# Hybrid decoder trunk, first token tiles: norm weight as one row, spread by two products over two PSUM banks

## Chip, cores and metric

One Trainium2 chip, one core. The metric is device time in microseconds of one execution, as the median of three runs. The engines are named as the profile names them: PE is TensorE (PEld its weight loads), DVE is VectorE, ACT is ScalarE, POOL is GpSimd, SP is SyncE. SBUF is the core's working memory, PSUM (eight banks of 128 x 512 float32) takes TensorE's results. Every engine works its own instructions off in order; semaphores make one wait for another.

## The reference, cut

```
for layer in range(2):
    h = rms_norm(x, norm_w[layer])                 # x: 256 tokens x 1024
    proj = einsum('bsd,de->bse', h, w_in[layer])   # 1024 x 12832
    ...
    x = x + einsum('bsd,de->bse', merged, w_out[layer])
return rms_norm(x, final_norm_w)

def rms_norm(x, w):
    return x * rsqrt(mean(x * x, axis=-1) + 1e-6) * w
```

Between the input projection and the output projection stand three mixers (a state-space scan, windowed attention, attention with forget gates). The change touches only the first layer's `rms_norm` and what leads from it to the first products of the projection.

## The kernel before

**Precision.** Dense products run in TensorE's faster float32 form. Each operand is split into a high part (a copy to that form) and a low part (the operand less its high part), and three products replace one: high x high, low x high, high x low. So every weight that is loaded needs one ScalarE copy (high) and one subtraction (low); tokens need the same.

**Tokens.** 256 tokens are two tiles of 128 rows, `x0[:, 0]` and `x0[:, 1]`, 1024 columns each, in two halves of 512. A tile is normalised, turned by TensorE against the identity matrix (four 128 x 128 turns into one PSUM bank for each half, line 278), and split out of that bank: high part by ScalarE (line 268), low part by VectorE (line 269). The results, `hTh` and `hTl`, hold eight k-steps of 128 channels; the first half gives k-steps 0 to 3, the second one 4 to 7.

**Weights.** The weights of a projection come as pieces of 256 or 512 columns. A piece of 256 columns has two parts of four k-steps, each one transfer of 512 KB into a `raw` buffer (line 345, on SyncE's queue; six buffers). The first two pieces belong to the keys and values of the windowed attention. Their four parts are split in pairs of k-steps (128 x 512): both high parts by ScalarE (line 1225), the first pair's low part by VectorE, the second pair's by GpSimd (line 1226, `tt` and `gtt`). Later parts are split whole (128 x 1024, lines 268 and 269, from a call of `split`).

**The start, lines 1211 to 1258.** Under `manual_schedule` the instructions of TensorE, VectorE, ScalarE and GpSimd keep the order in which the program issues them; the trace before shows them in that order. TensorE first does 30 turns of the identity (`WARM`, line 1215). The first tile's squares are summed in two halves, on VectorE (line 1231) and ScalarE (`sum_sq`, line 219). The root is GpSimd's power to -0.5 with one correcting step on VectorE (`rsqrt`, lines 204 to 214). VectorE scales the first tile by root and norm weight (line 1237) and it is turned. The second tile goes another way: ScalarE sums both halves of squares, GpSimd multiplies by the norm weight (lines 1239 and 1245), ScalarE scales by the root (lines 1251 and 1253).

**The first products.** `dense` (line 282) with `after` runs the first tile's 24 products of piece one in two groups of twelve, k-steps 0 to 3 and 4 to 7; in a group first the four high x high, then the four with the tokens' low part, then the four with the weights' low part. After each group of twelve it calls `second_rows(j)` (line 1246), which turns and splits half j of the second tile and then splits one part of piece two (`next(w1)`). The second tile's 24 products follow, k-step by k-step, three products each; then piece two for both tiles. From the third operation on only TensorE's order is by hand.

**Queues.** SyncE issues, in order: first tile (line 162), the norm weight copied to 128 rows (line 163), second tile (line 164), then six weight parts (line 1212, from line 345), and each further part when a raw buffer is free. ScalarE's own queue first has the table load for Exp (line 159).

Of the kernel before, what the change touches and what calls it, by code (L numbers as in the profile page):

```python
# [44 lines left out]
def hybrid_trunk(  # L45
# [17 lines left out]
    def T(tag, shape, dtype=F32, bufs=None):  # L63
        count[0] += 1
        return sb.tile(shape, dtype, tag=tag, name=f"{tag}_{count[0]}",
                       bufs=bufs if bufs is not None else BUFS.get(tag, 1))
# [32 lines left out]
    def transpose(o, a, i):  # L99
        clock["t"] += 0.109  # L100
        nc.tensor.transpose(o, a, i)  # L101
# [52 lines left out]
            print("drained", br, left, "at", round(clock["t"], 1))  # L154


    tab = T("tab", [P, 1])
    nc.vector.memset(tab, 0.0)
    act(tab, tab, AF.Exp)
    x0 = T("L8", [P, 2, D])  # L160
    nwb0 = T("nwb", [P, D])
    nc.sync.dma_start(x0[:, 0, :], x2[0:P, :])
    nc.sync.dma_start(nwb0, norm_w[0:1, :].to_broadcast([P, D]))  # L163
    nc.sync.dma_start(x0[:, 1, :], x2[P:S, :])
    ident = T("ident", [P, P])
    make_identity(nc, ident)
    tri = T("tri", [P, P])
# [36 lines left out]
    def rsqrt(v, n):  # L204

        r0 = T("sm", [P, 8])
        nc.gpsimd.tensor_tensor(r0[:, :n], v[:, :n], mhalf[:, :n], op=ALU.pow)
        a = T("sm", [P, 8])
        tt(a[:, :n], r0[:, :n], r0[:, :n], op=ALU.mult)
        tt(a[:, :n], a[:, :n], v[:, :n], op=ALU.mult)  # L210
        ts(a[:, :n], a[:, :n], -0.5, 1.5, op0=ALU.mult, op1=ALU.add)
        r = T("rs", [P, 8], bufs=4)
        tt(r[:, :n], r0[:, :n], a[:, :n], op=ALU.mult)
        return r
# [19 lines left out]
        stt(r[:, 0:1], a[:, 0:1], -3.0, r0[:, 0:1], op0=ALU.add, op1=ALU.mult)  # L234
        return r

    def row_rstd(ss, n):
        return rsqrt(row_var(ss, n), 1)

# [165 lines left out]
        y.l = l  # L405
        layers.append(y)
    y0 = layers[0]
    y0.nwb = nwb0

    pdma = pin(nc.scalar.dma_start)  # L410

# [682 lines left out]
            pump()  # L1094

    fin = {}

    def hT(y, t):
        if t == 0:
# [16 lines left out]
    def op(i, *fs):  # L1116
        for f in fs:
            ops.append((i, f))

    for y in layers:  # L1120
        l = y.l
        w = w_in[l]
        y.gate, y.qT, y.ckT, y.sz, y.yh, y.yl, y.sq, y.h, y.ss, y.var, y.zdone, y.cqdone = {}, {}, {}, {}, {}, {}, [], {}, {}, {}, set(), {}

        def cols(c0, n=256):
            return sub([(0, w[:, c0:c0 + n])], n)

        def z1(c0, br, b):
            op(cols(c0 + 256 * b), u_z(y, br, 2 * b, 0), u_z(y, br, 2 * b + 1, P))

        def zs(c0, br):
            for b in range(4):
                z1(c0, br, b)

        def gates_proj(br):
            def g(b):
                c = 512 * b
                op(cols(C_G + D * br + c, 512), u_gate(y, br, c, 0), u_gate(y, br, c, 1))

# [12 lines left out]
            return [lambda f=f, b=b: f(b) for f, b in seq]  # L1152

        if l == 0:
            k, v = cols(C_BK), cols(C_BV)
            op(k, u_bkv(y, 0, 0, [lambda j=j: second_rows(j) for j in range(2)]))
            op(k, u_bkv(y, 0, 1))
            op(v, u_bkv(y, 256, 0), u_bkv(y, 256, 1))
            op(None, lambda: layer_consts(y0))
            for c in (0, 2):  # L1160
                op(cols(C_BQ + 256 * c, 512), u_bq(y, c, 0), u_bq(y, c, 1))
        else:
            kv, q0 = cols(C_BK, 512), cols(C_BQ)
# [12 lines left out]
        gp = gates_proj(1)  # L1176
        lights = [lambda: None, lambda: op(cols(C_CV, 512), u_cv(y, 0, 0), u_cv(y, 0, 1))]
        lights += [lambda: None, lambda: op(cols(C_CV + 512, 512), u_cv(y, 512, 0), u_cv(y, 512, 1))]
        lights += [gp.pop(0), lambda: None, gp.pop(0), lambda: None]
        for (c0, u), light in zip(heavy, lights):  # L1180
            op(cols(c0), u_conv(y, u, 0), u_conv(y, u + 1, P))
            light()
        for f in gp:
            f()

        for b, zb in enumerate(((), (0,), (1,), (2, 3))):
            op(cols(C_CK + 256 * b), u_ck(y, 2 * b, 0), u_ck(y, 2 * b + 1, P))
# [23 lines left out]
    with tc.manual_schedule(engines={ENG.PE, ENG.DVE, ENG.Activation, ENG.Pool}):  # L1211
        load_to(N_RAW)
        warm = pmx()
        for i in range(WARM):
            transpose(warm[:, 0:P], ident, ident)
        ss = [T("ss", [P, 4], bufs=4) for _ in range(2)]
        h = [T("L4", [P, D]) for _ in range(2)]
        y0.hTh = T("L8", [P, NK // 2, 2, 2 * P], F32R)
        y0.hTl = T("L8", [P, NK // 2, 2, 2 * P], F32R)
        def shared():  # L1220
            for _ in range(2):
                raw, hi, lo = new_part()
                for k, sub_ in ((0, tt), (2, gtt)):
                    ks = slice(k, k + 2)
                    act(hi[:, ks, :], raw[:, ks, :], AF.Copy)  # L1225
                    sub_(lo[:, ks, :], raw[:, ks, :], hi[:, ks, :].bitcast(F32), op=ALU.subtract)  # L1226
                yield
        w0, w1 = shared(), shared()
        half = (slice(0, 512), slice(512, D))
        junk = T("L2", [P, 512])  # L1230
        nc.vector.tensor_tensor_reduce(out=junk, in0=x0[:, 0, half[1]], in1=x0[:, 0, half[1]], scale=1.0,
                                       scalar=0.0, op0=ALU.mult, op1=ALU.add, accum_out=ss[0][:, 1:2])
        sum_sq(x0, 0, 0, ss[0][:, 0:1], 512)
        r0 = row_rstd(ss[0], 2)
        sum_sq(x0, 1, 0, ss[1][:, 0:1], 512)
        for sl in half:
            stt(h[0][:, sl], x0[:, 0, sl], r0[:, 0:1], y0.nwb[:, sl], op0=ALU.mult, op1=ALU.mult)  # L1237
        sum_sq(x0, 1, 512, ss[1][:, 1:2], 512)
        gtt(h[1][:, half[0]], x0[:, 1, half[0]], y0.nwb[:, half[0]], op=ALU.mult)
        v1 = row_var(ss[1], 2)  # L1240
        to_hT(h[0], 0, y0.hTh, y0.hTl, (0,))
        r1 = rsqrt(v1, 1)
        next(w0)
        to_hT(h[0], 0, y0.hTh, y0.hTl, (1,))
        gtt(h[1][:, half[1]], x0[:, 1, half[1]], y0.nwb[:, half[1]], op=ALU.mult)
        def second_rows(j):
            with tc.high_priority():
                to_hT(h[1], 1, y0.hTh, y0.hTl, (j,))
            next(w1)

        act(h[1][:, half[0]], h[1][:, half[0]], AF.Copy, scale=r1[:, 0:1])
        next(w0)
        act(h[1][:, half[1]], h[1][:, half[1]], AF.Copy, scale=r1[:, 0:1])
        for i, f, _ in ops[:2]:
            f(pieces[i])
        pieces[0].last = True
        release(pieces[0], 2)
        run_op(*ops[2])
# [35 lines left out]
```

## Time and profile before

| | us |
|---|---|
| median of 3 runs (lowest to highest) | 832.72 (832.42 to 832.81) |
| the profiled execution: its time | 832.96 |
| the profiled execution: its span | 831.2 |
| TensorE busy in the span | 819.1 |
| VectorE, ScalarE, GpSimd busy | 654.2, 504.2, 121.1 |

A row of the timeline reads: start, duration from the first start to the last end, engine, line, operation, output <- inputs, shape, count (neighbours of one kind are merged), and in brackets how long the engine was idle before and what released it. A row of windows reads: stretch and its length, then busy time and count for PE, PEld, DVE, ACT and POOL, the granted clock of TensorE, the share of the transfer engines, GB/s. A row of a tile or line reads: line, engine, operation, count, then shortest, median and longest in ns, first and last start, forms. Records of matmuls are pipelined, and their ends are modelled. SPq and ACTq are the queues from which transfers are issued; the last figure of such a row on the page is the time from issue to landing.

### The profile page before, as it was taken

Reading aid. Unit: us, or ns where it says so; the run is one execution under the profiler, and the core shown is the slowest. Engines: PE = TensorE matmul, PEld = TensorE weight load, DVE = VectorE, ACT = ScalarE, POOL = GpSimd, SP = SyncE. Lnnn points to the kernel's source line nnn. Section 1 sums busy time; section 2 is a strip of 40 time slices with the busy share of each in tenths; the row PEclk is TensorE's granted clock in tenths of the full one; section 3 lists DMA queues with packets and bytes.
Section 4 is the critical chain, followed back from the end, with each engine's and each line's share of the span. In section 5 each row is a group of like instructions: output and inputs, shape, how many; then the busy total and the mean of one; then the engine's idle time right before and its main releaser. Section 6 shows DMA issues by size and latency. Waiting matters only on the chain.

```text
span 831.2 us, 15603 instructions
## 1 busy us (share of the span) xinstructions
PE 819.1 (99%) x5788; PEld 745.2 (90%) x5788; DVE 654.2 (79%) x1331; ACT 504.2 (61%) x972; POOL 121.1 (15%) x161
## 2 busy tenths in 40 slices
PE   7999999999999999999999999999999999999996
PEld 7999888989999998888989998898899999888896
DVE  5888987998776678875778889889968667888665
ACT  6566777655666676543555677775557666645442
POOL 7411300000130201100014131000003110021000
PEclk9999999999999999999999999999999999999999
DMA  9945565567474756675687465465756554577632
GB/s 301 275 146 184 179 203 165 171 222 222 134 208 133 247 165 191 215 227 191 210 242 218 148 212 172 144 188 200 239 167 182 173 178 153 167 224 230 215 104 74
DMA packets 123739, 158.39 MB, mean 191 GB/s; under 512 B 12800, under 2 KB 84208, under 8 KB 123664
## 3 DMA queue, kind: packets, MB, share of 16 engines
q1 hardware_dynamic: 109456, 140.79, 53.8%
q10 hardware_dynamic: 14160, 16.49, 6.5%
q8 instruction: 45, 0.74, 0.4%
q14 instruction: 30, 0.25, 0.1%
q0 software_dynamic: 48, 0.13, 0.0%
HBM read 155.22 MB, written 2.16 MB: 189 GB/s over the span
## 4 chain that ended last, share of the span: by engine, by line
PE 96%; DMA 2%; DVE 1%; issue 0%; ACT 0%; POOL 0%; SPq 0%; POOLq 0%; DVEq 0%
PE mm L97 81%; PE mx L97 11%; PE mx L101 4%; DMA raw<-in_w_in_dram 1%; DMA L<-in_x_dram 1%; POOL lo L1226 0%; DVE L L269 0%; DVE lo L269 0%; ACT hi L1225 0%; DVE L L1067 0%; ACT L L219 0%; ACT L L1084 0%; ACT L L268 0%; POOLq L1290 0%; SPq L163 0%
## 5 line engine op out<-in xcount | busy, mean ns | idle before, releaser
L269 DVE TENSOR_TENSOR lo<-raw,hi 128x1024 fp32r<-128x1024 f32 x252 | 309.9, 1244 | 71.8 <-ACT hi L268 69.4
L97 PE MATMUL mm<-hi,L 128*128 128x512 f32 (+1 forms) x1280 | 354.0, 363 | 2.1 <-ACT hi L1225 1.5
L97 PE MATMUL mm<-L,hi 128*128 128x256 f32 x1792 | 316.9, 278 | 0.0
L268 ACT ACTIVATE hi<-raw 128x1024 fp32r<-128x1024 f32 x252 | 263.1, 1055 | 78.2 <-PE mm L97 72.8
L97 PEld LDWEIGHTS mm<-L,hi 128*128 128x128 f32 x1792 | 277.5, 192 | 6.3 <-issue 3.7
L97 PEld LDWEIGHTS mm<-hi,L 128*128 128x128 f32 x1280 | 228.8, 189 | 32.1 <-issue 3.2
L97 PE MATMUL mm<-L,lo 128*128 128x256 f32 x896 | 246.4, 275 | 0.0
L97 PE MATMUL mm<-lo,L 128*128 128x512 f32 (+1 forms) x640 | 229.1, 359 | 1.4 <-POOL lo L1226 1.4
L97 PEld LDWEIGHTS mm<-L,lo 128*128 128x128 f32 x896 | 171.9, 192 | 0.2
L97 PEld LDWEIGHTS mm<-lo,L 128*128 128x128 f32 x640 | 120.9, 189 | 15.5 <-POOL lo L1226 1.8
L925 POOL TENSOR_SCALAR_AFFINE_SELECT bias<-bias 128x128 f32<-128x128 f32 x64 | 39.0, 642 | 268.2 <-DMA bias<-cumd 94.8
L779 DVE SCALAR_TENSOR_TENSOR L<-L,vec,L 128x255 f32<-128x255 f32 (+2 forms) x96 | 46.8, 487 | 6.9 <-ACT L L776 5.5
L949 ACT ACTIVATE L<-L 128x512 f32<-128x512 f32 x24 | 15.1, 630 | 38.9 <-DVE L L948 38.7
L97 PE MATMUL mx<-L,L 128*64 128x128 f32 (+1 forms) x384 | 36.5, 332 | 0.0
L97 PEld LDWEIGHTS mx<-L,L 128*64 128x64 f32 x384 | 23.8, 136 | 11.9 <-issue 2.7
L576 ACT ACTIVATE pp<-pp,nm 128x128 f32<-128x128 f32 x64 | 28.2, 443 | 8.3 <-DVE nm L570 8.3
L651 ACT ACTIVATE pp<-pp,nm 128x128 f32<-128x128 f32 x64 | 25.2, 394 | 12.9 <-DVE nm L644 12.8
L840 ACT ACTIVATE L<-mm 128x256 f32<-128x256 f32 x48 | 18.0, 375 | 20.5 <-PE mm L97 20.3
L782 ACT ACTIVATE L<-L 128x256 f32<-128x256 f32 x32 | 13.3, 416 | 24.4 <-DVE L L779 24.1
L676 POOL TENSOR_SCALAR_AFFINE_SELECT L<-L 128x256 f32<-128x256 f32 x16 | 10.2, 640 | 113.9 <-ACT L L674 113.9
L644 DVE CUSTOM_DVE_ANT_0 pp<-mx,wmask,nsink 128x128 f32<-128x128 f32 x64 | 24.2, 413 | 2.6 <-PE mx L97 2.6
L101 PE MATMUL mx<-ident,L 128*128 128x128 f32 x148 | 22.5, 275 | 0.3 <-DVE L L1237 0.3
(182 smaller groups left out, 795.9 us busy)
## 6 DMA issues: line engine op xcount, KB each, us to landing
raw<-in_w_in_dram SPq DMA_DIRECT2D x200, 512.0 KB, 4.6
raw<-in_w_proj_dram SPq DMA_DIRECT2D x48, 512.0 KB, 5.0
raw<-in_w_out_dram SPq DMA_DIRECT2D x16, 512.0 KB, 4.7
L<-cumd ACTq DMA_DIRECT2D x8, 512.0 KB, 3.7
bias<-cumd ACTq DMA_DIRECT2D x16, 256.0 KB, 3.6
L<-in_gate_bias_dram ACTq DMA_DIRECT2D x12, 256.0 KB, 3.7
L<-in_x_dram SPq DMA_DIRECT2D x2, 512.0 KB, 4.9
nwb<-in_norm_w_dram SPq DMA_DIRECT2D x1, 512.0 KB, 5.4
```

Of the source, the lines that this page charges most:

```text
L97: nc.tensor.matmul(o, a, b, **kw)
L101: nc.tensor.transpose(o, a, i)
L268: keep(act)(hi, src, AF.Copy)
L269: keep(tt)(lo, src, hi.bitcast(F32), op=ALU.subtract)
L576: act(pp[:, i, sl], pp[:, i, sl], AF.Exp, scale=-1.0, bias=nm[:, e:e + 1], accum_out=sums[:, e:e + 1])
L644: nc.vector.tensor_tensor_reduce(out=pp[:, i, sl], in0=score(p, i, b), in1=m, scale=-0.125, scalar=ns[:, i:i + 1], op0=ALU.add, op1=ALU.mi ...
L651: act(pp[:, i, sl], pp[:, i, sl], AF.Exp, scale=-1.0, bias=nm[:, e:e + 1], accum_out=sums[:, e:e + 1])
L779: stt(a[:, s:S], x_[:, 0:S - s], y.vec[:, 16 * j + u:16 * j + u + 1], a[:, s:S], op0=ALU.mult, op1=ALU.add)
L782: act(th, a, AF.Tanh)
L840: act(halves(th), p, AF.Tanh, scale=0.5)
L925: nc.gpsimd.affine_select(out=bias[:, i, dst], in_=bias[:, i, src], compare_op=ALU.is_ge, fill=NEG, base=0, pattern=[[-1, P]], channel_mul ...
L949: act(g, g, AF.Tanh, scale=0.5)
```

## The change

The norm weight of layer 0 arrives as one row of 1024 (4 KB), on ScalarE's queue, ahead of the table load. Behind the 30 turns TensorE multiplies a row of ones (1 x 128) with each half of it (1 x 512), in plain float32, into two PSUM banks `nwp`, so that all 128 rows hold the weight. VectorE reads it there when it scales, in place, and it scales both tiles now (`scaled`). GpSimd's and ScalarE's work on the second tile goes; the second tile's squares are summed by ScalarE and VectorE, as the first's. The epsilon enters with VectorE's sum of squares, and the root has one operation less ahead of the power and one less behind it. The second tile's transfer comes directly behind the first's. The order is written out: both halves of the first tile, its squares and root, then the second tile's squares, parts one and two of piece one, the second root, the second tile's scaling. Nothing happens after the first group of twelve products; after the second group `second_tile` turns both halves, and issues on ScalarE the high part of half one, the four copies of piece two's two parts, and the high part of half two; on VectorE both low parts of the tokens, and then piece two's low parts with GpSimd. `load_to(N_RAW + 2)` issues two more weight transfers ahead of these.

```diff
+    row = T("nwb", [P, D])
+    nc.scalar.dma_start(row[0:1, :], norm_w[0:1, :])
+    x0 = T("L8", [P, 2, D])
+    nc.sync.dma_start(x0[:, 0, :], x2[0:P, :])
+    nc.sync.dma_start(x0[:, 1, :], x2[P:S, :])
     tab = T("tab", [P, 1])
     nc.vector.memset(tab, 0.0)
     act(tab, tab, AF.Exp)
-    x0 = T("L8", [P, 2, D])
-    nwb0 = T("nwb", [P, D])
-    nc.sync.dma_start(x0[:, 0, :], x2[0:P, :])
-    nc.sync.dma_start(nwb0, norm_w[0:1, :].to_broadcast([P, D]))
-    nc.sync.dma_start(x0[:, 1, :], x2[P:S, :])
...
+    def first_root(ss):
+        v = T("sm", [P, 8])
+        ts(v[:, 0:1], ss[:, 0:1], ss[:, 1:2], 1.0 / D, op0=ALU.add, op1=ALU.mult)
+        r0 = T("sm", [P, 8])
+        nc.gpsimd.tensor_tensor(r0[:, 0:1], v[:, 0:1], mhalf[:, 0:1], op=ALU.pow)
+        return v, r0
+    def last_root(v, r0):
+        a = T("sm", [P, 8])
+        stt(a[:, 0:1], r0[:, 0:1], v[:, 0:1], r0[:, 0:1], op0=ALU.mult, op1=ALU.mult)
+        ts(a[:, 0:1], a[:, 0:1], -0.5, 1.5, op0=ALU.mult, op1=ALU.add)
+        r = T("rs", [P, 8], bufs=4)
+        tt(r[:, 0:1], r0[:, 0:1], a[:, 0:1], op=ALU.mult)
+        return r
...
-            op(k, u_bkv(y, 0, 0, [lambda j=j: second_rows(j) for j in range(2)]))
+            op(k, u_bkv(y, 0, 0, [lambda j=j: between[j]() for j in range(2)]))
...
+        nwp = [pmx() for _ in range(2)]
+        for p, sl in zip(nwp, half):
+            mm(p, ones[0:1, :], row[0:1, sl], start=True, stop=True)
...
+        def squares(t):
+            sum_sq(x0, t, 0, ss[t][:, 0:1], 512)
+            nc.vector.tensor_tensor_reduce(out=junk, in0=x0[:, t, half[1]], in1=x0[:, t, half[1]], scale=1.0,
+                                           scalar=D * EPS, op0=ALU.mult, op1=ALU.add,
+                                           accum_out=ss[t][:, 1:2])
+        def part():
+            raw, hi, lo = new_part()
+            def high(k):
+                act(hi[:, k:k + 2, :], raw[:, k:k + 2, :], AF.Copy)
+            def low(k, sub_):
+                sub_(lo[:, k:k + 2, :], raw[:, k:k + 2, :], hi[:, k:k + 2, :].bitcast(F32), op=ALU.subtract)
+            return high, low
+        def turned(t, j):
+            p = pmx()
+            for k in range(4):
+                transpose(p[:, k * P:(k + 1) * P], x0[:, t, j * 512 + k * P:j * 512 + (k + 1) * P], ident)
+            pv = p.rearrange("p (a t) -> p a t", a=2)
+            h, l = y0.hTh[:, 2 * j:2 * j + 2, t, :], y0.hTl[:, 2 * j:2 * j + 2, t, :]
+            return (lambda: act(h, pv, AF.Copy)), (lambda: tt(l, pv, h.bitcast(F32), op=ALU.subtract))
+        def scaled(t, j, r):
+            stt(x0[:, t, half[j]], x0[:, t, half[j]], r[:, 0:1], nwp[j], op0=ALU.mult, op1=ALU.mult)
+
+        squares(0)
+        r0 = last_root(*first_root(ss[0]))
+        scaled(0, 0, r0)
+        th0, tl0 = turned(0, 0)
+        scaled(0, 1, r0)
+        th1, tl1 = turned(0, 1)
+        squares(1)
+        h0, l0 = part()
+        h0(0)
+        th0()
+        h0(2)
+        tl0()
+        root = first_root(ss[1])
+        th1()
+        l0(0, tt)
+        l0(2, gtt)
+        h1, l1 = part()
+        h1(0)
+        h1(2)
+        r1 = last_root(*root)
+        tl1()
+        l1(0, tt)
+        l1(2, gtt)
+        scaled(1, 0, r1)
+        scaled(1, 1, r1)
+        low = []
+        def next_parts():
+            load_to(N_RAW + 2)
             for _ in range(2):
+                h, l = part()
+                h(0)
+                h(2)
+                low.append(l)
+        def second_tile():
+            parts = [turned(1, j) for j in range(2)]
+            parts[0][0]()
+            next_parts()
+            parts[1][0]()
+            for j in range(2):
+                parts[j][1]()
+            for l in low:
+                l(0, tt)
+                l(2, gtt)
+        between.extend([lambda: None, second_tile])
```

More of the change, by code (lines that the diff above doesn't have):

```diff
@@ L235, in row_rsqrt2 @@
         return r
-    def row_rstd(ss, n):
-        return rsqrt(row_var(ss, n), 1)
+    def first_root(ss):
[11 more added lines that the diff above has]
+        return r
     def in_turn(ap):
@@ L407, in hybrid_trunk @@
     y0 = layers[0]
-    y0.nwb = nwb0
     pdma = pin(nc.scalar.dma_start)
@@ L1096, in hybrid_trunk @@
     fin = {}
+    between = []
     def hT(y, t):
@@ L1215, in hybrid_trunk @@
             transpose(warm[:, 0:P], ident, ident)
+        half = (slice(0, 512), slice(512, D))
+        nwp = [pmx() for _ in range(2)]
+        for p, sl in zip(nwp, half):
+            mm(p, ones[0:1, :], row[0:1, sl], start=True, stop=True)
         ss = [T("ss", [P, 4], bufs=4) for _ in range(2)]
-        h = [T("L4", [P, D]) for _ in range(2)]
         y0.hTh = T("L8", [P, NK // 2, 2, 2 * P], F32R)
         y0.hTl = T("L8", [P, NK // 2, 2, 2 * P], F32R)
-        def shared():
-            for _ in range(2):
[L1222 to L1249, printed above, removed]
@@ L1251, in hybrid_trunk @@
-        act(h[1][:, half[0]], h[1][:, half[0]], AF.Copy, scale=r1[:, 0:1])
-        next(w0)
-        act(h[1][:, half[1]], h[1][:, half[1]], AF.Copy, scale=r1[:, 0:1])
+        junk = T("L2", [P, 512])
+        def squares(t):
[3 more added lines that the diff above has]
+                                           accum_out=ss[t][:, 1:2])
```

## The prediction

> **What bounds the kernel now.** I read the page's busy shares first, then the chain of waits, then the windows of the span, and last the timeline of the first 20 us, engine by engine.
>
> ```profile
> span 831.2 us, 15603 instructions
> PE 819.1 (99%) x5788; PEld 745.2 (90%) x5788; DVE 654.2 (79%) x1331; ACT 504.2 (61%) x972; POOL 121.1 (15%) x161
> ...
> 10.00:20.00 10.00, 7.85 (x59) 7.18 (x60) 6.54 (x16) 8.54 (x15) 7.80 (x6) 1.00 1.00 337
> 20.00:30.00 10.00, 10.00 (x75) 9.47 (x74) 9.60 (x10) 6.46 (x10) 5.92 (x5) 1.00 0.94 267
> 30.00:60.00 30.00, 30.00 (x198) 27.11 (x197) 22.50 (x65) 17.26 (x44) 7.59 (x8) 1.00 0.60 187
> 60.00:400.00 340.00, 340.00 (x2439) 309.12 (x2438) 272.35 (x545) 210.33 (x400) 40.77 (x54) 1.00 0.60 189
> 400.00:800.00 400.00, 399.45 (x2829) 363.17 (x2828) 322.10 (x651) 246.92 (x476) 51.63 (x67) 1.00 0.63 196
> ```
>
> TensorE is the bound. From 20 to 800 us it is idle for 0.55 us. So whatever the start gains or loses reaches the end one to one, as long as the start only shifts TensorE's queue. The question is when that queue begins to run without a hole. In the chain of waits this is near 17 us:
>
> ```profile
> 2.18 7.81 DMA raw<-in_w_in_dram
> ...
> 10.01 1.16 ACT hi L1225 x2
> ...
> 14.67 1.29 POOL lo L1226
> 15.96 0.04 issue
> 16.00 0.51 PE mm L97 x2
> 16.51 0.43 PE mx L101 x4
> 16.94 8.35 PE mm L97 x72
> ```
>
> The first weights land at 9.99; then ScalarE's high parts and GpSimd's low parts hold TensorE, until the second tile's last turn at 16.35. The last hole of the start is in the second tile's 24 products:
>
> ```profile
> 16.35 0.60 PE L101 MATMUL mx<-ident,L 128*128 128x128 f32 x4
> 16.98 0.60 ACT L268 ACTIVATE L<-mx 128x512 fp32r<-128x512 f32 x1
> 17.48 1.14 ACT L1225 ACTIVATE hi<-raw 128x512 fp32r<-128x512 f32 x2
> 17.61 0.69 DVE L269 TENSOR_TENSOR L<-mx,L 128x512 fp32r<-128x512 f32 x1 [0.34 <-ACT L L268]
> ...
> 18.11 0.28 PE L97 MATMUL mm<-lo,L 128*128 128x256 f32 x1
> 18.23 0.52 PE L97 MATMUL mm<-hi,L 128*128 128x256 f32 x2
> ```
>
> The second half of that tile is turned (16.35), its high part copied (16.98 to 17.58) and its low part formed (to 18.30). The second of the two products at 18.23, the first one that reads that low part, starts 0.28 us (one product's time, the row above it) before the pair's end: 18.23 + 0.52 - 0.28 = 18.47. **My sum is the shift of this instruction**, the product of the second tile's fifth k-step with the tokens' low part; behind it TensorE has all it needs.
>
> **What is removed.** The broadcast norm weight (512 KB, second in SyncE's queue) goes, and 4 KB come on ScalarE's queue.
>
> ```profile
> nwb<-in_norm_w_dram SPq DMA_DIRECT2D x1, 512.0 KB, 5.4
> ...
> 1.24 0.43 SPq L163 DMA_DIRECT2D nwb<-in_norm_w_dram  x1
> ...
> 8.07 0.63 ACT L219 ACTIVATE L<-L 128x512 f32<-128x512 f32 x1 [2.98 <-DMA L<-in_x_dram]
> ```
>
> It landed at 1.24 + 5.4 = 6.64, the second tile at about 8.0. So second tile and weights come some 1.4 us earlier: about 6.6, and 8.6 for the first weights. If that wait stayed the bound, this would be the gain. The issue of the 4 KB stands ahead of ScalarE's table load, whose result is wanted at 4.37 only; cover more than 1.5 us. Even if it took as long as the second tile does now (8.0 - 1.7 = 6.3), it is there at 7.1, before TensorE asks. The two 512 KB issues that are added wait, as the later ones do now, for a raw buffer: nothing. GpSimd's two weight products, one square and two scalings on ScalarE go; none of them is in my chain except through what replaces them.
>
> **The two row products.** They stand behind the 30 warming turns in TensorE's queue.
>
> ```profile
> L101 PE MATMUL mx<-ident x30: 273/417/473, 1.5 to 7.3; 128*128 128x128 f32 x30
> L97 PE MATMUL mx<-L,qt x128: 269/374/378, 52.6 to 527.0; 64*128 64x128 f32 x64, 64*128 64x256 f32 x64
> L97 PE MATMUL mx<-L x32: 272/327/382, 156.6 to 637.8; 128*128 128x256 f32 x16, 128*128 128x128 f32 x16
> 156.48 0.73 PEld L97 LDWEIGHTS mx<-L 128*128 128x128 f32 x4
> 157.14 0.19 PEld L97 LDWEIGHTS mm<-L,hi 128*128 128x128 f32 x1
> ```
>
> The last turn starts at 7.31, so TensorE is free at about 7.42. A full float32 product is two records (line 813 issues 8 products of 256 columns, the group counts 16). Here 256 + 128 columns took 157.14 - 156.48 = 0.66 us, so 512 take 0.88; by the starts of the products instead it is 0.77. Fewer rows do not help as far as the rows show: 64 rows have 378 ns where 128 have 382. A one-row product is in no row; its bounds are 0.2 (as if the rows counted) and 0.88; I take 0.88, the row nearest to it, since half the rows saved nothing. Bank one is done at 8.30. From a product's passage to its reader's start go 0.2: four turns take 0.60 and one at least 0.273, so they start 0.11 apart, the last one at 16.68, passes in 0.11 and is read at 16.98. So **bank one is read at 8.50, bank two at 9.38**.
>
> The first root is ready long before: one small operation of 0.2 less ahead of GpSimd's power and one less behind it, so at 6.6 instead of 7.02 (6.86 + 0.16 below). The banks decide.
>
> ```profile
> 4.37 0.69 DVE L1231 CUSTOM_DVE_ANT_0 L<-L 128x512 f32<-128x512 f32 x1 [3.44 <-DMA L<-in_x_dram]
> 6.86 0.16 DVE L213 TENSOR_TENSOR rs<-sm,sm 128x1 f32<-128x1 f32 x1
> 7.06 1.41 DVE L1237 SCALAR_TENSOR_TENSOR L<-L,rs,nwb 128x512 f32<-128x512 f32 x2
> 9.86 0.55 POOL L207 TENSOR_TENSOR sm<-sm,mhalf 128x1 f32<-128x1 f32 x1 [0.27 <-DVE sm L224]
> ```
>
> **VectorE's line behind the banks**, in program order: scaling (two at 1.41, so 0.66 from start to start and 0.75 each): 8.50 to 9.25 and, with bank two, 9.38 to 10.13. Then the second tile's square, 10.04 to 10.73 (0.69, the first row), which waited behind the scalings though its tokens are there since 6.6. The first low part of the tokens 10.75 to 11.44 (0.69; its high part ends at 10.5: turned 9.31, read 9.94). The variance, 11.36 to 11.51. The weights' low part, first pair, 11.44 to 12.13. Power on GpSimd, asked for at 11.6.
>
> **Where VectorE and GpSimd meet.** These rows price GpSimd's pairs of 512:
>
> ```profile
> 11.18 0.69 DVE L1226 TENSOR_TENSOR lo<-raw,hi 128x512 fp32r<-128x512 f32 x1
> 11.24 1.78 POOL L1226 TENSOR_TENSOR lo<-raw,hi 128x512 fp32r<-128x512 f32 x1 [0.82 <-ACT hi L1225]
> ...
> 12.81 0.76 DVE L1226 TENSOR_TENSOR lo<-raw,hi 128x512 fp32r<-128x512 f32 x1 [0.34 <-ACT hi L1225]
> 12.98 1.73 POOL L1245 TENSOR_TENSOR L<-L,nwb 128x512 f32<-128x512 f32 x1
> 14.67 1.28 POOL L1226 TENSOR_TENSOR lo<-raw,hi 128x512 fp32r<-128x512 f32 x1
> ```
>
> Alone it takes 1.28. With a VectorE operation of two SBUF inputs under way it ends 1.15 after that one (11.87 to 13.02, 13.57 to 14.71). VectorE in its turn started at 12.81, met GpSimd's end at 13.02 and ended 0.55 behind it. They take turns and wait each other out.
>
> Applied here: the power (0.55, of which 1.28 - 1.15 = 0.13 runs before the turn) is asked for during the weights' low part and ends at 12.13 + 0.42 = 12.55. GpSimd goes straight on to the first pair's low part, 12.53 to 13.81, while VectorE has the second root's three small operations next, two of them with two SBUF inputs. The first gets its turn at 13.81, the third waits for GpSimd's next pair, 13.95 to 15.10. Root at 15.2. No row shows so small an operation waiting; the bounds are no wait at all (root at 13.1, three starts of 0.19 behind 12.55) and the whole of both pairs. I take the whole, since the operations of 512 waited whole. Then in VectorE's queue: token low part 15.20 to 15.89, weights' low part to 16.51, scalings of the second tile to 17.18 and 17.84. [...]
>
> **The order behind it.** TensorE's 24 products of the first tile end with the part from 16.51, at 17.0. Then both halves of the second tile are turned, one behind the other, where one was turned in the middle before: first one 17.23, read at 17.86. Now ScalarE: high part, then **four** copies of the next two weight parts, then the other half's high part.
>
> ```profile
> 15.37 0.58 ACT L268 ACTIVATE L<-mx 128x512 fp32r<-128x512 f32 x1
> 15.85 1.14 ACT L1225 ACTIVATE hi<-raw 128x512 fp32r<-128x512 f32 x2
> ```
>
> Starts are 0.48 apart behind a turn's copy, 0.52 within the pair (1.14 - 0.62). So 17.86 + 0.49 + 4 x 0.52 = 20.43; before, two copies lay between. Copied at 21.03, low part 21.06 to 21.75, product 0.17 later: 21.92, against 18.47. **The shift is 3.45 us: 832.96 + 3.45 = 836.4 for a profiled execution**, which stood 0.24 above the median of the runs; so **836.2** as a median. Later demands stay covered: the second piece's low parts are ready at 22.4 and 23.1, TensorE takes them from 23.2; VectorE's three rope operations and GpSimd's two sums move by as much as TensorE does.
>
> **Rivals.**
> *The small operations don't wait.* The root is there at 13.1, the tokens' low part at 13.8, and only the weights' low part and GpSimd's last pair take turns, in one order or the other: the last parts are ready at 15.7 to 16.0, the second tile's first turn starts at 15.9 to 16.4 instead of 17.23, and the shift is 2.1 to 2.6; at 2.4 the time is 835.1. For: no row shows a small one waiting. Against: the operation at 12.81 did.
> *No turns at all in this place.* The power ends at 12.2, GpSimd's pairs take 1.5 each (between 1.28 and 1.78) and end at 15.2, and by the path above the product comes 5.0 later, at 20.2: shift 1.7, 834.4. Against: both orders of waiting stand in the rows.
> *A cheap row product.* At 0.2 each the banks are read at 7.8 and 8.1; the second scaling starts 0.66 behind the first, at 8.5 instead of 9.38. With whole waits the shift is 2.6, 835.3; with no turns 0.8, 833.5. Against it speaks the 64-row row.
> *The earlier weights decide (not slower).* The place is the landing of the first weights, 9.99 now and 8.6 then. It decides if the banks are read before 7.06, where scaling starts today, so that all the work behind them meets its weights 1.4 us earlier: 831.3. For: the chain starts with that DMA. Against: the banks come behind 30 turns that end past 7.3, and ScalarE's queue has the copies ahead of the last high part.
> *More holes.* If TensorE's waits (12.4 to 13.9, 14.7 to 15.9) leave half a microsecond that I don't see, 836.7.
> That the change does nothing can't be: ScalarE's order alone is two copies (1.04 us) longer ahead of the last high part.
>
> **How the numbers follow.** Whole waits 0.43 (836.2), small ones don't wait 0.20 (835.1), no turns 0.13 (834.4), cheap product 0.12 (0.07 of it 835.3, 0.05 of it 833.5), more holes 0.04, earlier weights 0.08 (831.3). A measurement of this kernel tells 0.2% from no change, 1.7 us: 831.1 to 834.4. "No turns" lies on that edge and is halved; "earlier weights" lies 0.2 inside the other and goes 0.05 out, 0.03 in. So slower 0.43 + 0.20 + 0.06 + 0.07 + 0.04 = 0.80, within 0.15, faster 0.05. The range runs from "no turns" with products at 0.77 (834.2, and some of the cheap ones) to more holes with their few tenths: 833.9 to 836.9; outside are the earlier weights and the cheapest case, 0.13, and what lies above.
>
> **What would show it.** Scaling starts at about 8.5, on TensorE, and not at 6.7; the second root's small operations held up until about 15.2, some 2.6 us behind GpSimd's power; GpSimd's two pairs back to back from 12.5; the second tile's second high part at 20.4 on ScalarE behind four copies; TensorE's unbroken run from about 21.9. I am wrong if scaling starts at 7, if the second root takes under 0.7 us behind the power, or if a wait on TensorE beyond 25 us appears.

## The result and the profile after

| | before | after |
|---|---|---|
| median of 6 runs each (lowest to highest), us | 832.78 (832.42 to 833.05) | 836.15 (835.90 to 836.42) |
| the profiled execution: time, span, us | 832.96, 831.2 | 836.0, 834.2 |

The changed kernel takes 1.0041 of the time before, with an interval of 1.0031 to 1.005; the medians differ by 3.4 us, the two spans by 3.0. Of all runs below one is set apart, a run of experiment 3 that took 1423.32 us at a mean granted clock of 0.557; that row's highest time and ratio leave it out. The head of the page and the windows of the changed kernel (stretch, length, busy time and count of PE, PEld, DVE, ACT, POOL, granted clock, share of the transfer engines, GB/s):

```profile
span 834.2 us, 15604 instructions
...
10.00:20.00 10.00, 7.58 (x41) 6.39 (x40) 6.71 (x11) 4.06 (x9) 4.12 (x4) 0.83 0.76 257
...
60.00:400.00 340.00, 340.00 (x2436) 308.95 (x2435) 272.91 (x552) 212.41 (x411) 39.66 (x54) 1.00 0.62 191
400.00:800.00 400.00, 399.51 (x2843) 363.61 (x2843) 323.09 (x652) 246.82 (x476) 51.71 (x67) 1.00 0.63 194
```

From 60 to 800 us TensorE is idle for 0.49 us, where it was 0.55 before. So nothing was lost late, and the whole difference lies in the start. One number was not there before: a mean granted clock of 0.83 between 10 and 20 us, where the kernel before had 1.00 in its profiled execution. The timeline of the start, all engines, with the rows that answer to the prediction's steps (start, duration, engine, line, operation, output <- inputs, shape, count, idle time before and its releaser):

```profile
1.51 4.93 PE L101 MATMUL mx<-ident 128*128 128x128 f32 x30 [1.51 <-POOL ident masks.py:199]
6.37 1.98 PE L97 MATMUL mx<-nwb,ones 1*128 1x512 f32 x4
7.40 0.63 ACT L1249 ACTIVATE hi<-raw 128x512 fp32r<-128x512 f32 x1 [0.78 <-DMA raw<-in_w_in_dram]
7.53 1.61 DVE L1264 SCALAR_TENSOR_TENSOR L<-L,rs,mx 128x512 f32<-128x512 f32 x2 [0.51 <-PE mx L97]
9.68 1.49 PE L97 MATMUL mm<-hi,L 128*128 128x256 f32 x8
10.55 0.93 POOL L242 TENSOR_TENSOR sm<-sm,mhalf 128x1 f32<-128x1 f32 x1 [4.17 <-DVE sm L240]
11.45 2.54 POOL L1252 TENSOR_TENSOR lo<-raw,hi 128x512 fp32r<-128x512 f32 x2
11.52 1.24 DVE L248 SCALAR_TENSOR_TENSOR sm<-sm,sm 128x1 f32<-128x1 f32 x1 [0.45 <-POOL sm L242]
12.98 1.03 DVE L251 TENSOR_TENSOR rs<-sm,sm 128x1 f32<-128x1 f32 x1
14.67 1.20 PE L97 MATMUL mm<-hi,L 128*128 128x256 f32 x4 [0.89 <-DVE L L1261]
15.14 1.40 DVE L1264 SCALAR_TENSOR_TENSOR L<-L,rs,mx 128x512 f32<-128x512 f32 x2
15.67 1.05 PE L97 MATMUL mm<-lo,L 128*128 128x256 f32 x4
16.52 1.83 PE L101 MATMUL mx<-ident,L 128*128 128x128 f32 x8
17.61 0.60 ACT L1261 ACTIVATE L<-mx 128x512 fp32r<-128x512 f32 x1 [5.94 <-PE mx L101]
18.11 2.18 ACT L1249 ACTIVATE hi<-raw 128x512 fp32r<-128x512 f32 x4
20.18 0.58 ACT L1261 ACTIVATE L<-mx 128x512 fp32r<-128x512 f32 x1
21.55 0.39 PE L97 MATMUL mm<-hi,L 128*128 128x256 f32 x1 [0.34 <-DVE L L1261]
```

Read it from the bottom. The product that the prediction followed starts at 21.55, against 18.47 before: a shift of 3.08 for a span that grew by 3.0. It waits for the second low part of the second tile on VectorE, and that for the high part (20.18), which stands behind four copies (18.11). These stand behind the first high part (17.61) and the turns (16.52). The turns follow the first tile's last eight products in TensorE's queue (14.67, 15.67); the scaling (15.14) is done with its first half at about 15.9 and doesn't hold them. The eight products wait 0.89 us for a low part of the tokens, which stands on VectorE behind the second root, and two of that root's three small operations last 1.24 and 1.03 us while GpSimd works on its two pairs (11.45 to 13.99). The first weights (7.40) are there well before TensorE can use them.

The clock has its own rows, in windows of half a microsecond (length, PE busy and count of records, granted clock, share of the transfer engines, GB/s):

```profile
4.00:4.50 0.50, 0.50 (x4) 1.00 0.99 401
4.50:5.00 0.50, 0.50 (x7) 1.00 0.96 383
...
14.50:15.00 0.50, 0.33 (x1) 0.73 0.99 344
...
18.00:18.50 0.50, 0.50 (x4) 0.85 0.26 94
```

A window whose clock is 0.73, between 1.00 and 0.50, was at half pace for 54% of its length. The windows left out have 1.00 up to 14.5 and 0.50 from 15.0 to 18.0. So the fall is at 14.73, and by the same reckoning the rise is at 18.15: 3.42 us at half pace, right where the second tile is turned.

### The profile page after: what moved, and what is told of

Same layout as the page of the kernel before. It is cut to its first block, busy times and chain, and to the rows that moved or that the text cites. A ratio compares the mean times of both kernels' runs of the same rounds, so it can differ in the third digit from the quotient of the medians.

```text
span 834.2 us, 15604 instructions
## 1 busy us (share of the span) xinstructions
PE 822.2 (99%) x5792; PEld 746.3 (89%) x5792; DVE 657.6 (79%) x1331; ACT 502.3 (60%) x968; POOL 116.6 (14%) x159
## 3 DMA queue, kind: packets, MB, share of 16 engines
HBM read 154.70 MB, written 2.16 MB: 188 GB/s over the span
## 4 chain that ended last, share of the span: by engine, by line
PE 97%; DVE 1%; issue 1%; ACT 0%; DMA 0%; POOL 0%; POOLq 0%; DVEq 0%
PE mm L97 82%; PE mx L97 11%; PE mx L101 4%; DMA L<-in_x_dram 0%; DVE L L1261 0%; POOL sm L242 0%; DVE sm L248 0%; ACT L L1261 0%; ACT hi L1249 0%; ACT L L1097 0%; DVE L L283 0%; DVE L L1241 0%; ACT L L282 0%; POOLq L1349 0%; ACT L L219 0%
## 5 line engine op out<-in xcount | busy, mean ns | idle before, releaser
L97 PEld LDWEIGHTS mm<-lo,L 128*128 128x128 f32 x640 | 121.2, 190 | 15.2 <-POOL lo L1252 1.4
```

Source lines behind the costliest of these rows:

```text
L97: nc.tensor.matmul(o, a, b, **kw)
```

## The experiments

Edits 1 to 8 are made to the changed kernel, 9 and 10 to the kernel of 8; each has 4 to 11 runs. Three groups of them (1 to 4, 5 to 8, 9 to 11) each stood beside the kernel before on their own chip; its median there was 832.65, 832.79 and 832.64 us, so the groups can be laid side by side. The profiles below are of one execution each, and the place of the half clock and the time at which the banks are read differ from one to the next: what an edit gains is read from the medians, and the profile shows which wait is gone.

| | median, us (lowest to highest) | ratio to before | interval |
|---|---|---|---|
| the change | 836.15 (835.90 to 836.42) | 1.0041 | 1.0031 to 1.0050 |
| 1 first small operation | 835.09 (834.10 to 835.47) | 1.0026 | 1.0016 to 1.0037 |
| 2 both small operations | 834.98 (834.30 to 835.61) | 1.0027 | 1.0017 to 1.0037 |
| 3 copies last | 834.91 (834.57 to 835.38) | 1.0026 | 1.0016 to 1.0037 |
| 4 filling turns | 835.81 (835.22 to 837.05) | 1.0038 | 1.0023 to 1.0053 |
| 5 earlier root | 834.32 (833.25 to 834.96) | 1.0016 | 1.0007 to 1.0026 |
| 6 = 2 and 3 | 833.85 (833.21 to 834.45) | 1.0012 | 1.0002 to 1.0021 |
| 7 twenty turns | 835.40 (834.82 to 835.74) | 1.0031 | 1.0019 to 1.0042 |
| 8 all in order | 831.53 (830.84 to 832.69) | 0.9985 | 0.9976 to 0.9994 |
| 9 = 8, 128 rows | 831.18 (830.44 to 832.32) | 0.9982 | 0.9973 to 0.9991 |
| 10 = 8, twenty turns | 832.17 (830.25 to 832.39) | 0.9984 | 0.9975 to 0.9993 |
| 11 = 8 again | 831.07 (830.54 to 832.40) | 0.9983 | 0.9974 to 0.9992 |

The ratio is not the quotient of the two medians; in 10, whose runs fall into two groups, that quotient is 0.9994. The intervals of 1, 2, 3 and 7 overlap that of the change, but none of the runs that they rest on reaches its lowest one, 835.90.

**1. The first small operation without a second tensor.** It multiplies r0 by v and by r0; here both factors come in as one scalar for each row, and only one operand is read as a tensor.

```diff
-        stt(a[:, 0:1], r0[:, 0:1], v[:, 0:1], r0[:, 0:1], op0=ALU.mult, op1=ALU.mult)
+        ts(a[:, 0:1], r0[:, 0:1], v[:, 0:1], r0[:, 0:1], op0=ALU.mult, op1=ALU.mult)
```

> Changed kernel, but the first of the second root's three small VectorE operations has one tensor input and two per-row scalars instead of two tensor inputs. Theory (two SBUF tensor inputs make a VectorE operation wait out GpSimd's pair, however small it is): the first no longer waits (1.24 us now), the third waits for the end of the first pair only, the root is ready at about 12.8 instead of 14.0, the second tile is turned at about 15.2 instead of 16.5: 1.2 to 1.7 us faster than the changed kernel, 834.5 to 834.9. Rival (the operations are late for another reason, the power's result or the pointers): 836.1, the first one still takes 1.2 us.

The timeline of the second root in experiment 1:

```profile
11.93 0.93 POOL L242 TENSOR_TENSOR sm<-sm,mhalf 128x1 f32<-128x1 f32 x1 [5.72 <-DVE sm L240]
12.83 2.55 POOL L1252 TENSOR_TENSOR lo<-raw,hi 128x512 fp32r<-128x512 f32 x2
12.89 0.27 DVE L248 TENSOR_SCALAR sm<-sm,sm 128x1 f32<-128x1 f32 x1 [0.45 <-POOL sm L242]
...
13.38 0.75 DVE L251 TENSOR_TENSOR rs<-sm,sm 128x1 f32<-128x1 f32 x1
```

The same value at the same place, while GpSimd works on its pair: 0.27 where the other form took 1.24. The third operation, left as it was, waits out the first pair only (to 14.13). The root is there 1.27 behind the power's end at 12.86, and not 2.53 as in the change (11.48 to 14.01). In this execution the banks came late (scaling from 8.90), so the times of day are not those of the change. The median fell by about 1 us, a little less than expected. So the waits are real and are paid on the path.

**2. Neither small operation with a second tensor.**

```diff
-        stt(a[:, 0:1], r0[:, 0:1], v[:, 0:1], r0[:, 0:1], op0=ALU.mult, op1=ALU.mult)
+        ts(a[:, 0:1], r0[:, 0:1], v[:, 0:1], r0[:, 0:1], op0=ALU.mult, op1=ALU.mult)
...
-        tt(r[:, 0:1], r0[:, 0:1], a[:, 0:1], op=ALU.mult)
+        ts(r[:, 0:1], r0[:, 0:1], a[:, 0:1], None, op0=ALU.mult)
```

> Changed kernel, with the first and the third of the root's small operations in the form with one tensor input. Theory: none of them waits, root at about 12.0, GpSimd's second pair ends at 14.4, the second tile is turned at 14.9: 2.1 us faster than the changed kernel, 834.0, and TensorE's granted clock may then stay at full. Rival: 836.1.

This was missed by half. The timeline of experiment 2, the power and then VectorE from the third small operation on:

```profile
11.86 0.93 POOL L242 TENSOR_TENSOR sm<-sm,mhalf 128x1 f32<-128x1 f32 x1 [5.54 <-DVE sm L240]
...
13.32 0.21 DVE L251 TENSOR_SCALAR rs<-sm,sm 128x1 f32<-128x1 f32 x1
...
14.05 1.81 DVE L1252 TENSOR_TENSOR lo<-raw,hi 128x512 fp32r<-128x512 f32 x1
15.78 1.39 DVE L1264 SCALAR_TENSOR_TENSOR L<-L,rs,mx 128x512 f32<-128x512 f32 x2
```

The root now takes 0.74 behind the power (12.79 to 13.53). But the weights' low part behind it, 0.68 alone, lasts 1.81: VectorE meets GpSimd's second pair there instead. The scaling starts at 15.78, in experiment 1 at 15.86. The wait had moved by one instruction, so that the second repair brought nothing (834.98 against 835.09). Nor did the clock stay at full: in this execution it is at half from 10.57 to 13.98.

**3. The copies of the next weights behind the second high part.**

```diff
             parts[0][0]()
-            next_parts()
             parts[1][0]()
+            next_parts()
```

> Changed kernel, with the high part of the second tile's second half ahead of the four copies on ScalarE. Theory (the four copies delay the last low part): the high part starts at 18.1 instead of 20.2, the product that needs the last low part at 20.5 instead of 21.55, bounded by TensorE's own pace then: 1.05 us faster, 835.1. Rival (the four copies are needed as early, the later piece is the bound): the wait moves to the second piece's products, 836.1.

ScalarE and TensorE in experiment 3:

```profile
18.43 0.60 ACT L1261 ACTIVATE L<-mx 128x512 fp32r<-128x512 f32 x1 [0.26 <-PE mx L101]
...
18.95 0.39 PE L97 MATMUL mm<-hi,L 128*128 128x256 f32 x1 [0.22 <-DVE L L1261]
...
20.36 0.40 PE L97 MATMUL mm<-hi,L 128*128 128x256 f32 x2
```

The high part that began at 20.18 begins at 18.43, and TensorE has no hole behind 18.95. The time fell by 1.1 to 1.2 us: the order on ScalarE is a cause of its own. It isn't the full 1.75, because TensorE now has the products of four k-steps to do first, from 18.95 on, about as late as in the change. The product that was followed, the second of the two at 20.36, starts at 20.48 (20.36 + 0.40 - 0.28), 1.07 before 21.55, as expected.

**4. Ten turns of the identity in the empty place between the groups of twelve.** They are to keep the clock up.

```diff
-        between.extend([lambda: None, second_tile])
+        def filler():
+            for i in range(10):
+                transpose(warm[:, 0:P], ident, ident)
+
+        between.extend([filler, second_tile])
```

> Changed kernel, with ten more turns of the identity into the spare bank behind the first twelve products, in a hole of TensorE (13.1 to 14.7). Theory (the half clock from 14.8 to 18.2 comes from the hole ahead of it, and costs 1.0 us on the path, as much as the row products came earlier than I put them): the granted clock stays at 1.0, the second tile's turns take 1.0 us instead of 1.8, 835.1. Rival (the half clock comes from something else, or is off the path): 836.1.

The first tile's last four products, the second tile's turns and the product that ends the start, in experiment 4:

```profile
15.60 0.74 PE L97 MATMUL mm<-lo,L 128*128 128x256 f32 x4
16.31 1.33 PE L101 MATMUL mx<-ident,L 128*128 128x128 f32 x8
...
20.91 0.39 PE L97 MATMUL mm<-hi,L 128*128 128x256 f32 x1 [0.34 <-DVE L L1261]
```

In this execution the granted clock was 1.00 in every window of the start; the turns take 1.33 and not 1.83, and the product starts 0.64 earlier than in the change, though the row products start 0.37 later (6.74). The median of four runs is only 0.3 lower, and the interval covers that of the change. So in these two executions the half clock costs time on the path, where it falls on the turns; that filling turns mend it over many executions isn't shown.

**5. The second root ahead of the pairs.**

```diff
-        r0 = last_root(*first_root(ss[0]))
+        root = first_root(ss[0])
+        squares(1)
+        r0 = last_root(*root)
+        root = first_root(ss[1])
         scaled(0, 0, r0)
         th0, tl0 = turned(0, 0)
         scaled(0, 1, r0)
         th1, tl1 = turned(0, 1)
-        squares(1)
+        r1 = last_root(*root)
...
-        root = first_root(ss[1])
...
-        r1 = last_root(*root)
```

> Changed kernel, with the second tile's squares, variance and power ahead of the first tile's scaling, in the hole in which VectorE waits for the row products, and its root's small operations directly behind the scalings. Theory (the wait for the row products costs because the second root stands behind it, and the small operations then meet GpSimd's pairs): no small operation waits, the power is off the path, the second tile is turned at about 14.4 instead of 16.5, 1.8 to 2.4 us faster than the changed kernel: 833.7 to 834.3. Rival (the pairs of 512 alone hold the line): the gain stays at that of the earlier runs, about 1.0, 835.1.

Experiment 5, the operations with unchanged form but another place:

```profile
8.61 1.60 DVE L1264 SCALAR_TENSOR_TENSOR L<-L,rs,mx 128x512 f32<-128x512 f32 x2 [1.43 <-PE mx L97]
10.13 0.21 DVE L248 SCALAR_TENSOR_TENSOR sm<-sm,sm 128x1 f32<-128x1 f32 x1
...
10.56 0.16 DVE L251 TENSOR_TENSOR rs<-sm,sm 128x1 f32<-128x1 f32 x1
...
11.34 1.79 DVE L1252 TENSOR_TENSOR lo<-raw,hi 128x512 fp32r<-128x512 f32 x1
...
15.74 1.33 PE L101 MATMUL mx<-ident,L 128*128 128x128 f32 x8
```

0.21 and 0.16 for the very instructions that took 1.24 and 1.03: it was the meeting that was dear. GpSimd is met again by the weights' low part (1.79), but the turns start at 15.74 and not at 16.52, though the banks came 1.1 later in this execution (scaling from 8.61). Part of that is the clock, which is at full here by then: the turns take 1.33 and not 1.83. The time fell by 1.8 us, in relation to before from 1.0041 to 1.0016.

**6. Experiments 2 and 3 together.**

> Changed kernel with both edits: the root's small operations with one tensor input, and the copies behind the last high part. Theory (two terms, one behind the other on one path): the gains add, 1.2 + 1.2, 833.8. Rival (each uncovers the same other wait): 834.9.

833.85, 2.3 us below the change, where 2 and 3 alone brought some 1.1 each. The causes add up. What is left to before is 1.1 us; no run takes that apart.

**7. Twenty warming turns for thirty.**

```diff
-WARM = 30
+WARM = 20
```

> Changed kernel with 20 warming turns instead of 30, so that the row products stand 10 turns earlier in TensorE's queue. Theory (VectorE's scaling waits for the products alone): scaling starts at the root, 7.05, and bank two is there: 0.6 us faster, 835.5, more where the clock rises late. Rival (with fewer turns the clock rises later and the products run at half speed): scaling starts at 8 to 9, 836.1 or more.

First the scaling, then two windows of TensorE in experiment 7:

```profile
7.28 1.61 DVE L1264 SCALAR_TENSOR_TENSOR L<-L,rs,mx 128x512 f32<-128x512 f32 x2 [0.28 <-PE mx L97]
```

```profile
9.50:10.00 0.50, 0.50 (x4) 0.72 1.09 344
...
16.50:17.00 0.50, 0.50 (x6) 0.95 0.61 164
```

Scaling starts at 7.28, near the theory's 7.05, and the time, 0.8 below that of the change, is near its 835.5. The banks are read 0.25 earlier than in the profile of the change, whose turns sped up early (at some 4.5 us), and 1.62 earlier than in that of experiment 1. Against this the clock is at half from 9.72 to 16.55, which is 6.83 us, twice 3.42, as the rival had it in kind. What each of the two is worth can't be told from this run.

**8. Everything at once.** The small operations as in experiment 2, the second root early, the weights' first low part ahead of it on VectorE, each half of the second tile scaled early and turned behind one of the two groups of twelve as the kernel before did, and the copies of piece two last.

```diff
         h0(0)
+        l0(0, tt)
         th0()
         h0(2)
+        l0(2, gtt)
+        r1 = last_root(*root)
         tl0()
-        root = first_root(ss[1])
+        scaled(1, 0, r1)
         th1()
-        l0(0, tt)
-        l0(2, gtt)
...
+        def first_half():
+            th, tl = turned(1, 0)
+            th()
+            tl()
+
+        def second_half():
+            th, tl = turned(1, 1)
+            th()
+            tl()
             load_to(N_RAW + 2)
...
-        between.extend([lambda: None, second_tile])
+        between.extend([first_half, second_half])
```

> Changed kernel in another order: second root early, small operations with one tensor input, the weights' first low part on VectorE ahead of the root and asked for before GpSimd's, the second tile's first half scaled and turned between the two groups of twelve products, the copies of the second piece last. Theory (every term of the sum is an order, and the row products themselves are cheap): TensorE runs without a hole from about 14.2, the product that stood at 18.47 before the change comes at 15.8: 2.7 us faster than before, 830.0. Rival (the row products' place and the pairs of 512 keep the start as late as before): 832.5.

The windows and TensorE's timeline in experiment 8:

```profile
9.00:9.50 0.50, 0.50 (x4) 0.63 1.09 346
...
12.50:13.00 0.50, 0.50 (x6) 0.95 1.05 385
```

```profile
6.97 1.98 PE L97 MATMUL mx<-nwb,ones 1*128 1x512 f32 x4
...
10.60 2.16 PE L97 MATMUL mm<-hi,L 128*128 128x256 f32 x8
...
13.07 0.60 PE L101 MATMUL mx<-ident,L 128*128 128x128 f32 x4
...
15.32 0.63 PE L101 MATMUL mx<-ident,L 128*128 128x128 f32 x4
```

This kernel beats both: 831.53, and 831.07 when it was run again (11), 1.3 to 1.6 us below before. TensorE is busy all but without a hole from the first products on, and each half is turned behind one group of twelve (13.07, 15.32). The expected time was 1.5 lower. In this execution the clock is at half from 9.13 to 12.55, and the first eight products take 2.16 where eight took 1.49 in the change. That isn't all of it: the runs of 8 and 11 whose clock stood highest still have a median of 830.84, against the 830.0 expected.

**9 to 11. The row products in 128 rows, twenty turns, and the same once more.** In 9 the row stands in a zeroed tile and is multiplied in all 128 rows by ones; 10 has 20 turns, by the edit of 7; 11 is experiment 8 unchanged.

```diff
+    nc.vector.memset(row, 0.0)
...
-            mm(p, ones[0:1, :], row[0:1, sl], start=True, stop=True)
+            mm(p, ones, row[:, sl], start=True, stop=True)
```

> The reordered kernel, with the two row products as products of 128 rows: all rows of the norm weight's tile are zeroed first (VectorE), row 0 is loaded, and the ones have 128 rows. Same two products of 512 columns, same result. Theory (a product of one row keeps TensorE busy in the records, but does not count as work for its clock: in every run with the late rise the half clock follows the row products by one or two us): the granted clock no longer falls to 0.5 between 9 and 13 us, and the first 24 products of the tokens run at full pace: 0.5 to 1.0 faster than the reordered kernel, 830.6 to 831.0. Rival (the fall comes from the hole behind, or zeros count no more than missing rows): the fall stays, 831.5.

> The reordered kernel with 20 warming turns. Theory (VectorE's scaling waits for the products, also in this order): scaling starts at about 7.2 instead of 8.1, 0.4 to 0.9 faster than the reordered kernel, 830.6 to 831.1. Rival (fewer turns leave the clock at half for longer and take it back): 831.5 or more, with granted clock at 0.5 through two windows, as in the run with ten turns less.

> The reordered kernel once more, as the mark for the other two on one chip: 831.5, ratio to the kernel before 0.9985.

The row products in experiment 9, then in experiment 10:

```profile
7.64 1.88 PE L97 MATMUL mx<-nwb,ones 128*128 128x512 f32 x4
```

```profile
5.98 3.77 PE L97 MATMUL mx<-nwb,ones 1*128 1x512 f32 x4
```

128 rows cost 1.88, one row costs 1.98: rows make no difference to the price. To the clock they seem to: each run also gives its mean granted clock over the span (a block of 3.42 us at half lowers it by 0.002, and one can fall into the idle end too, as in the profile of before, which is at 0.50 from 830.0 on). In 8 and 11 together, 8 of 21 runs have 0.995, with a median of 831.77, and 5 have 0.999, with one of 830.84; in 9 all eleven lie between 0.997 and 0.999. This isn't proof: the kernel before, which has no row products, shows 0.995 or 0.996 in 8 of its 27 runs beside them. And the median of 9 is no better, 831.18 against 831.07; why is open. Experiment 10 misses: its runs fall into two groups, five from 830.25 to 831.26 and six from 832.17 to 832.39, and the profiled one, 832.21, has its row products at half pace (3.77, against 1.98 in 8), and the turns ahead of them keep to 4 or 5 records in each half microsecond from 4.0 to their end at about 6.0. That the fewer turns are the cause is the author's estimate: experiment 7, also with twenty, has row products of 2.12.

## Why the prediction was right

| step | predicted | measured |
|---|---|---|
| row products start | 7.42 | 6.37 |
| bank two is read after bank one | 0.88 | 0.86 (7.53 + 1.61 - 0.75 = 8.39) |
| scaling of the first tile | 8.50 | 7.53 |
| root behind the power's end | 2.65 (12.55 to 15.2) | 2.53 (11.48 to 14.01) |
| scaling of the second tile | 16.51 | 15.14 |
| its first turn, first copy | 17.23, 17.86 | 16.52, 17.61 |
| second high part behind the first | 2.57 | 2.57 (17.61 to 20.18) |
| the product that ends the start | 21.92 | 21.55 |
| shift of it | 3.45 | 3.08 |

**The small operations.** They wait, and for the whole pair each (1.24 and 1.03 us, against 0.21 and 0.16 in experiment 5): the choice that the prediction made between bounds of nothing and both pairs. Experiment 1 takes one of the waits away by its form, experiment 5 both by their place, and the time falls with them. With two tensors the first operation of 128 x 1 took 1.24 while GpSimd worked on its pair; with one tensor and two scalars it took 0.27 at the same place. But what the waits cost is not their sum. Experiment 2 shows that the next operation with two SBUF inputs waits in their place (1.81, against 0.68 alone), and 1.2 us are gained (836.15 to 834.98). The prediction's rival of small ones that don't wait had this price, 1.1 (836.2 to 835.1), since it let the low part take turns with GpSimd; the expectation for experiment 2 did not.

**The copies on ScalarE.** Step and size were right, 0.49 + 4 x 0.52; experiment 3 shows that they are on the path.

**The row products.** One row costs as much as 128 (1.98 and 1.88 for the two products), as taken, so the rival of a cheap one falls. Their start was off for this execution: "TensorE is free at about 7.42" was read from one execution, and in the profile of the change the turns sped up at some 4.5 us, in that of before at some 7.0. So the banks, and all that follows on VectorE down to the root, came about 1 us earlier than put, and scaling at 7.53 is nearer to the prediction's own sign of being wrong (7) than to its 8.5. In experiments 1, 2 and 5, which leave the turns and the row products as they were, it begins at 8.90, 8.84 and 8.61. So this start moves from execution to execution, and one trace can't give it.

**The clock.** It isn't in the sum; the rival of more holes put half a microsecond for something unseen. The half clock from 14.73 to 18.15 holds up the first tile's last products and the second tile's turns. Four products with the weights' low part take 1.05 (0.74 at full pace in experiment 4), and from the second tile's first turn to its copy go 1.09, where the prediction took 0.63. The path differs there too: in the prediction the first turn waits for the scaling (16.51 to 17.23), in the profile for these products. Against the prediction the second tile's scaling comes 1.37 early, the copy behind its turns only 0.25: some 1.1 us of the lead are gone in between, most of it by the clock. So in this execution two errors of about 1 us each nearly cancelled, and 836.2 was as close to 836.15 as it was partly by luck. The two big terms, waits and copies, were not luck: experiment 6 takes off what these two edits can reach of both, and 2.3 of the 3.4 us go with them.

**The earlier weights.** They came at 7.40 (at 8.48 in experiment 2), earlier than the 8.6 put, and TensorE's first products stood behind other work, so the side on which the change could have been faster never came into reach. Experiment 8, without the waits, the copies and the late turns in the second tile's path, is 1.3 to 1.6 us faster than before, about as much as the weights were put earlier (1.4). That this is their saving isn't shown: no run gives the kernel before the new order and leaves its weights where they were.

## What to carry to other kernels

A transfer that comes earlier is worth what the queue behind it can use (here the copy of the first weights started at 7.40 instead of 10.01, and the kernel took 3.4 us longer): list the instructions that stand between it and the bound engine, in program order, and price each at the place where it now falls. Look for VectorE's operations with two SBUF tensors in the time in which GpSimd works, the small ones too: here one of 128 x 1 took 1.24 us there and 0.21 elsewhere, and 0.27 there with its other operands as scalars for each row; then look which instruction meets GpSimd next. Copies for the next piece belong behind the last piece of work that the bound engine is waiting for (experiment 3: 836.15 to 834.91).

## What was not expected of the hardware

In these traces the granted clock goes in blocks of 3.42 us. In the profile of the change it falls at 14.73 and rises at 18.15; counted back by 3.42 this gives 11.31, 7.89 and 4.47, and at about 4.5 the warming turns double their pace (4 records in the window from 4.0, 7 in that from 4.5), though the recorded clock says 1.00 on both sides. In experiment 7 it is at half for two blocks (9.72 to 16.55), in 8 for one (9.13 to 12.55). In the block ahead of the fall in the change, 11.31 to 14.73, TensorE worked for 1.36 of 3.42 us (to 11.62, 12.79 to 13.78, and 0.06 at the end, behind a wait of 0.89). TensorE's timeline of the change, then that of the kernel before with one of its windows, which had the longer single hole (1.51 against 1.17) and kept its clock in this execution:

```profile
11.12 0.50 PE L97 MATMUL mm<-lo,L 128*128 128x256 f32 x2
12.79 0.51 PE L97 MATMUL mm<-lo,L 128*128 128x256 f32 x2 [1.17 <-POOL lo L1252]
13.14 0.64 PE L97 MATMUL mm<-hi,L 128*128 128x256 f32 x4
```

```profile
10.70 1.50 PE L97 MATMUL mm<-hi,L 128*128 128x256 f32 x8 [1.51 <-ACT hi L1225]
```

```profile
10.00:10.50 0.50, 0.00 (x0) 1.00 1.10 348
```

So the length of one hole alone does not decide. In experiment 8 the block ahead of the fall, 5.71 to 9.13, has TensorE busy from end to end by the records, 1.98 us of it with the products of one row. Experiment 9, with 128 rows, shows no fall at the start. The clock does not fall behind every stretch of one-row products: in the change itself 1.5 us of them fill the end of the block from 4.47 to 7.89, behind 1.9 us of turns, and the clock stays. The theory of experiment 9, that a product of one row doesn't count as work for the clock, fits these traces and the mean clocks of 8, 9 and 11 (0.995 in 8 of the 21 runs of 8 and 11, 0.997 to 0.999 in the eleven of 9), but isn't shown; what brings the clock down stays open.
